# A two-layer S5 and gMLP trunk: the opening laid out anew, the S5 periods given less projection work, five y tiles prepared inside them

## The chip, the core and the metric

The kernel runs on one core of one Trainium2 chip. A core has five engines that run side by side, each through its own instructions in program order: TensorE (PE in the profile; its weight loads are PEld), VectorE (DVE), ScalarE (ACT), GpSimd (POOL) and SyncE (SP). An instruction that waits on a semaphore holds up everything behind it on its engine. DMAs are issued here by SP and, for a few transfers, by ScalarE; a DMA instruction also holds its engine until what it waits for has come. The metric is the device time of one execution in microseconds. The kernel before took 875.73 us (median of 3 runs, 874.96 to 876.68).

## What is computed

The reference runs two layers over a sequence of 1024 frames of 1024 features, all in float32, and a last rmsnorm:

```python
for i in range(DEPTH):                       # DEPTH = 2
    h = rmsnorm(x, norm_g[i])
    if i % 2 == 0:                           # S5 layer
        branch, gate = split(h @ s5_w_in)    # 1024 x 2048
        y = gelu(s5_mixer(branch, ...))      # 64 groups of 16 channels, 64 complex states each
        y = y * sigmoid(y @ w_glu + b_glu)
        out = (y * silu(gate)) @ s5_w_out
    else:                                    # gMLP layer
        u, v, gate = split(h @ sgu_w_in)     # 1024 x 3072
        out = (sgu_mixer(gelu(u), gelu(v), ...) * silu(gate)) @ sgu_w_out
    x = x + out
return rmsnorm(x, final_g)
```

The mixer is `h_t = lam_bar * h_(t-1) + b_bar @ u_t`, `y_t = Re(C h_t) + D u_t`, with a complex diagonal `lam_bar` that depends on the weights alone.

## The kernel before

Every large product is made from operands split in two float32r parts (hi and lo), with three matmuls for each tile of 128 rows: hi by hi, hi by lo, lo by hi. `w_split` makes the parts of a weight panel: a ScalarE copy (w_hi) and a subtraction on VectorE or GpSimd (w_lo).

The opening. x comes in two halves of 512 frames (tiles xh). `x_turn` transposes one 128-feature block of a half on TensorE (four transposes), `x_hi` copies it with the norm weight (ScalarE), `x_lo` takes the rest (VectorE); the results are ahi and alo. `in_mm(i, half, ks)` runs the matmuls of weight panel i against one half of the frames, one step for each of eight blocks k. The rms factor of a frame is multiplied in at the eviction (`in_out`, tile rb); `x_square`, `rsqrt` and `x_factor` make it for all eight blocks at once. Between these stand the operations on the mixer's parameters on VectorE (`decay`, `angles`, `powers`, taken one at a time by `pull`), and on GpSimd the phases (`phases`), the first table of rotations (`tab_ops(0)`, tile e) and the products of beta and B (`beta_b`, written to device memory as b_d and read back for each batch).

The S5 periods. The 64 groups are worked in 16 units of 4. `period(p)`, for p from -3 to 16, does one stage of several units, so that they overlap: kernel generation for unit p+3 (`gen_ops`, tiles wn and xn), transposes and the Toeplitz kernel for unit p+2 (`w_turn`, `k_mm`, `k_skip` into tile kpad, `k_store` from kpad to t_d), the recurrence of unit p, and the output product of unit p-1 (`out_mm`). The recurrence is a rotation by a table cs (`rot_co` on VectorE, `rot_si` on GpSimd), a real scan along time, and the rotation back. cs is a piece of e, brought by two SP DMAs in `load_cs`. All engines keep the order of the program text here. Into each period TensorE gets steps of the input projection as filling: `FILL` says how many at five places (11 in all; `FILL0` 6, for p below 0). In the periods `mm` takes steps from a list, `evict` runs one eviction, `split` one weight split, `queue` one weight load and one store; only two PSUM banks hold projection results then.

The tail. Units write their outputs to y_d. Each of 8 y tiles is loaded by eight DMAs (`load_y`), passed through gelu (`y_gelu`, ScalarE) and split (`y_split`, VectorE). `EARLY` of them (3) are prepared inside the last periods, the others behind them; then comes the gate product (w_glu), and the rest of the kernel, which the change leaves as it is. Both the y tiles and the gelu results use a pair of buffers (`ctile`) while the periods run.

Of the kernel before, what the change touches and what calls it, by code (L numbers as in the profile page):

```python
# [36 lines left out]
FILL = (3, 2, 2, 2, 2)  # L37
FILL0 = (2, 1, 1, 1, 1)
JR = 32
EARLY = 3  # L40
# [20 lines left out]
def trunk(ctx, tc, x, norm_g, final_g, s5_w_in, A_re, A_im, log_dt, B_re, B_im, C_re, C_im,  # L61
# [165 lines left out]
    b_d = drp.tile([KT, P, 8 * JR], F32, name="b_d")  # L227
# [3 lines left out]
    cnat = xp.tile([P, KT, 3, NS], F32, name="cnat")  # L231
    anat = tmp((G, 4, NS))
# [8 lines left out]
    ea = held.tile([P, 2, G], F32, name="ea")  # L241

# [31 lines left out]
    junk = stp.tile([P, D], F32, name="junk", tag="st")  # L274
# [5 lines left out]
    def x_factor(r):  # L280

        for half in range(2):
            ps = auxps()
            for b in range(4):
                dr = xp.tile([P, P], F32, name="dr", tag="dr", bufs=2)
                S.activation(dr, ident, AF.Copy, scale=r[:, half * 4 + b:half * 4 + b + 1])
                T.matmul(ps[:, b * P:(b + 1) * P], lhsT=ones, rhs=dr, start=True, stop=True)
            S.activation(rb[:, half * HALF:(half + 1) * HALF], ps, AF.Copy)
# [16 lines left out]
    def in_mm(i, half, ks):  # L305
        if ks[0] == 0:
            in_ps[i, half] = mmps()
        hi, lo = in_w[i]
        cs = slice(half * HALF, (half + 1) * HALF)
        for k in ks:  # L310
            mm3(in_ps[i, half], (hi[:, k], lo[:, k]), (ahi[:, k, cs], alo[:, k, cs]), k == 0, k == KT - 1)
# [118 lines left out]
    br, bi = tmp(), tmp()  # L430

    def vmul(orr, oi, ar_, ai_, br_, bi_, t, t2):
# [6 lines left out]
        yield tt(oi, oi, t2, ALU.add)  # L439

    def powers():

        l1r, l1i = lp[:, 0, :, 1], lp[:, 1, :, 1]
        tb, tc_ = tmp((P, G, L)), tmp((P, G, L))
        yield tt(l1r, ea[:, 0], cth[:, 0:G], ALU.mult)
        yield tt(l1i, ea[:, 0], sth[:, 0:G], ALU.mult)

        def beta():
            den, nr, t1, t2 = tmp(), tmp(), tmp(), tmp()
            yield tt(den, ar, ar, ALU.mult)  # L450
            yield tt(t1, ai, ai, ALU.mult)
# [64 lines left out]
    NB = {"wn": 2, "b0": 2, "xn": 5, "wt": 3, "e": 2, "cs": 3, "hh": 2, "traw": 3, "us": 4}  # L516
    tabs, wns, wts, xns, b0s, css, tts, us, hhs, gqs, rots, s1s, ggs, out_ps = ({} for _ in range(14))
# [206 lines left out]
    S.activation(warm, warm, AF.Square)  # L724
    Q.dma_start(g0, norm_g[0].rearrange("(k p) -> p k", p=P))
# [5 lines left out]
    w_load(1, xp.tile([P, KT, P], F32, name="raw_x"))  # L731
    load_x(1, 0, 2, 0, D)
    load_x(1, 2, 4, 0, D)
    load_bc()
# [27 lines left out]
    ps_a = auxps()
    for i in range(2):
        T.transpose(ps_a[:, i * G:(i + 1) * G], anat[:, 2 * i:2 * i + 2].rearrange("p a b -> p (a b)"), ident[0:G, 0:G])
    x_lo(0, 0)
    x_lo(0, 1)
    ts(ar, ps_a[:, 0:G], RE_CLIP, None, ALU.min)
    V.tensor_copy(ai, ps_a[:, G:2 * G])
    pull(2)
    x_lo(0, 2)  # L770
    pull(2)
    x_lo(0, 3)
    pull(2)
    w_split(0, V)
# [3 lines left out]
    x_square(0)  # L778
    x_square(1)
    pull(14)  # L780
    for k in range(4, 8):
# [8 lines left out]
    pull(64)  # L790
    phases()
    for _ in tab_ops(0):
        pass
    steps = powers()
# [8 lines left out]
    x_square(6)
    x_square(7)
    ts(xv, ss, 1.0 / D, RMS_EPS, ALU.mult, ALU.add)
    r = rsqrt(xv, KT, lambda: pull(1))
    x_factor(r)
    in_mm(1, 1, range(0, 4))
    c_turn(0)
    pull(8)  # L810
# [4 lines left out]
    w_load(2)
    in_mm(1, 1, range(4, 8))
    c_turn(1)
    pull(99)
    S.activation(bs, bs, AF.Copy, scale=sgn[:, 0:1])
    beta_b()  # L820
    w_split(2, V)
# [12 lines left out]
    todo = [(i, half, k) for i in range(2, 16) for half in range(2) for k in range(KT)]  # L834
    outs, splits, loads, stores = [], [3], [], []
# [39 lines left out]
    def period(p):  # L875
# [5 lines left out]
        if p % 2 == 0 and 2 <= p + 4 < 16:  # L881
            tab.append(tab_ops((p + 4) // 2))
# [43 lines left out]
        split()  # L926
# [13 lines left out]
    load_b0(0)  # L940
# [20 lines left out]
    for k in range(EARLY, KT):  # L961
        mm(5)
# [248 lines left out]
```

## Time and profile before

| | us |
|---|---|
| median of 3 runs | 875.73 |
| the profiled execution | 875.46 |
| its span (first to last instruction) | 873.7 |
| PE busy | 828.5 |
| DVE busy | 505.0 |
| ACT busy | 287.0 |
| POOL busy | 227.1 |

The span holds 10905 instructions; TensorE's mean granted clock is 0.977 of full speed. The chain of work that ended last is put down to PE for 76% of the span, DVE 12%, DMA 5%, ACT 3%. These are means over stages with different limits. A helper records each operation, so all instructions of the kernel carry one line number (L74) and are told apart by their tiles: mm is a projection product, aux another TensorE product, rot and cs the rotation, gg the scan's result, c a y tile or its gelu. The SP and ACT queues (SPq, ACTq) show DMAs by the time that issuing takes.

### The profile page before, as it was taken

To read this page: it belongs to the slowest core of one execution; us is meant where nothing else is said; L and a number is where in the kernel's file an instruction comes from. 1 tells how busy PE (TensorE), PEld (TensorE's weight loads), DVE (VectorE), ACT (ScalarE), POOL (GpSimd) and SP (SyncE) were. 2 spreads that over 40 slices of the span, in tenths; PEclk is the share of its full clock that TensorE was granted. 3 is DMA by queue.
4 is the path that set the end of the run, shared out by engine and by line. 5 is a ranking of instruction groups with operands and counts; after the bars stand their busy time and mean duration, and the time that the engine had idled before them with its cause. 6 is when DMAs were issued, how large, how long until landed. Compare 5 with 4: busy or idle time off the path is not lost.

```text
span 873.7 us, 10905 instructions
## 1 busy us (share of the span) xinstructions
PE 828.5 (95%) x3946; PEld 671.6 (77%) x3946; DVE 505.0 (58%) x1101; ACT 287.0 (33%) x519; POOL 227.1 (26%) x241
## 2 busy tenths in 40 slices
PE   5766999999999989999999999999999899999996
PEld 3555788888888768888888888888888688888884
DVE  5986788787744686665157511211399954462255
ACT  3622343443344564444112321311321122242122
POOL 1463776676542000000000000000036721212221
PEclk9978999999999979999999999999999999999999
DMA  9504887978877573456011321210310011371022
GB/s 255 74 26 126 219 230 199 254 190 222 213 181 180 139 236 97 145 168 217 25 73 72 121 73 49 97 48 1 97 49 0 25 49 32 137 225 40 2 97 96
DMA packets 124326, 104.35 MB, mean 119 GB/s; under 512 B 20592, under 2 KB 105584, under 8 KB 124272
## 3 DMA queue, kind: packets, MB, share of 16 engines
q1 hardware_dynamic: 114368, 97.29, 39.4%
q10 hardware_dynamic: 9904, 6.36, 2.3%
q8 instruction: 31, 0.51, 0.2%
q14 instruction: 23, 0.19, 0.1%
HBM read 68.50 MB, written 26.21 MB: 108 GB/s over the span
## 4 chain that ended last, share of the span: by engine, by line
PE 76%; DVE 12%; DMA 5%; ACT 3%; SPq 2%; issue 1%; POOL 1%; ACTq 0%; POOLq 0%
PE mm L74 67%; PE aux L74 7%; DVE lo L74 4%; SPq L74 2%; PE rot L74 1%; DMA c<-y_d 1%; DMA raw<-in_sgu_w_in 1%; DVE alo L74 1%; DVE t L74 1%; DMA raw<-in_s_w_in 1%; ACT c L74 1%; DVE rs_y L74 1%; DVE rs_t L74 1%; DVE stats L74 1%; DVE c L74 1%
## 5 line engine op out<-in xcount | busy, mean ns | idle before, releaser
L74 PE MATMUL mm<-ahi,w_hi 128*128 128x512 f32 x512 | 212.3, 415 | 4.9 <-ACT w_hi L74 4.1
L74 PE MATMUL mm<-ahi,w_lo 128*128 128x512 f32 x512 | 205.9, 402 | 3.1 <-DVE w_lo L74 3.1
L74 PE MATMUL mm<-alo,w_hi 128*128 128x512 f32 x512 | 204.6, 400 | 0.7 <-DVE alo L74 0.6
L74 PEld LDWEIGHTS mm<-ahi,w_hi 128*128 128x128 f32 x512 | 98.9, 193 | 26.7 <-ACT w_hi L74 4.6
L74 PEld LDWEIGHTS mm<-ahi,w_lo 128*128 128x128 f32 x512 | 98.6, 193 | 26.4 <-DVE w_lo L74 4.8
L74 PEld LDWEIGHTS mm<-alo,w_hi 128*128 128x128 f32 x512 | 99.0, 193 | 21.5 <-DVE alo L74 2.3
L74 PE MATMUL mm<-c,ahi 128*128 128x512 f32 x256 | 80.3, 395 | 0.0
L74 DVE TENSOR_TENSOR w_lo<-raw,w_hi 128x1024 fp32r<-128x1024 f32 x26 | 38.0, 1461 | 69.3 <-ACT w_hi L74 69.2
L74 POOL TENSOR_TENSOR lo<-lo,lnb 128x128 f32<-128x128 f32 x64 | 34.4, 566 | 162.1 <-DVE lo L74 162.1
L74 ACT ACTIVATE w_hi<-raw 128x1024 fp32r<-128x1024 f32 x39 | 41.1, 1054 | 82.1 <-PE mm L74 54.4
L74 DVE TENSOR_TENSOR c<-mm,c 128x512 f32<-128x512 f32 x32 | 22.0, 690 | 67.0 <-PE mm L74 67.0
L74 POOL TENSOR_SCALAR_AFFINE_SELECT wsn<-wsn 128x1024 f32<-128x1024 f32 x1 | 1.1, 1093 | 221.3 <-DMA wsn<-in_sgu_w_s 221.3
L74 PEld LDWEIGHTS mm<-c,ahi 128*128 128x128 f32 x256 | 48.1, 188 | 11.6
L74 PE MATMUL mm<-hi,w_hi 128*128 128x512 f32 x128 | 52.1, 408 | 2.8 <-DVE hi L74 1.7
L74 PE MATMUL mm<-lo,w_hi 128*128 128x512 f32 x128 | 52.7, 412 | 1.0 <-DVE lo L74 0.9
L74 PE MATMUL mm<-hi,w_lo 128*128 128x512 f32 x128 | 51.6, 404 | 0.0
L74 PE MATMUL mm<-hi,alo 128*128 128x512 f32 x128 | 51.0, 399 | 0.0
L74 PE MATMUL mm<-hi,ahi 128*128 128x512 f32 x128 | 50.7, 396 | 0.0
L74 PE MATMUL mm<-ahi,hi 128*128 128x512 f32 x128 | 50.6, 396 | 0.0
L74 PE MATMUL mm<-lo,ahi 128*128 128x512 f32 x128 | 50.6, 395 | 0.0
L74 PE MATMUL mm<-alo,hi 128*128 128x512 f32 x128 | 50.6, 395 | 0.0
L74 PE MATMUL mm<-c,alo 128*128 128x512 f32 x128 | 50.5, 395 | 0.0
(162 smaller groups left out, 1458.3 us busy)
## 6 DMA issues: line engine op xcount, KB each, us to landing
raw<-in_sgu_w_in SPq DMA_DIRECT2D x24, 512.0 KB, 3.7
cs<-e SPq DMA_DIRECT2D x32, 256.0 KB, 5.7
raw<-in_s_w_in SPq DMA_DIRECT2D x15, 512.0 KB, 4.5
u_d<-stage SPq DMA_DIRECT2D x8, 512.0 KB, 5.2
us<-u_d SPq DMA_DIRECT2D x16, 256.0 KB, 5.3
t_d<-kpad SPq DMA_DIRECT2D x64, 64.0 KB, 3.2
traw<-t_d SPq DMA_DIRECT2D x16, 256.0 KB, 5.5
y_d<-ysb ACTq DMA_DIRECT2D x16, 256.0 KB, 3.3
```

The lines of the kernel that those rows point to most:

```text
L74: ins = getattr(self.engine, name)(*args, **kwargs)
```

## The change

The constants and the order of work change; a few tiles move to other pools, and the beta products stay on chip.

```diff
-FILL = (3, 2, 2, 2, 2)
-FILL0 = (2, 1, 1, 1, 1)
+FILL = (2, 2, 2, 2, 1)
+FILL0 = (2, 2, 2, 1, 1)
+WARM = 16
-EARLY = 3
+EARLY = 5
...
+    def x_scale(half, r):
+        drs = [xp.tile([P, P], F32, name="dr", tag=f"dr{b}") for b in range(4)]
+        for b in range(4):
+            S.activation(drs[b], ident, AF.Copy, scale=r[:, b:b + 1])
+        return drs
+
+    def x_factor(half, drs):
+        ps = auxps()
+        for b in range(4):
+            T.matmul(ps[:, b * P:(b + 1) * P], lhsT=ones, rhs=drs[b], start=True, stop=True)
+        S.activation(rb[:, half * HALF:(half + 1) * HALF], ps, AF.Copy)
...
         for k in ks:
-            mm3(in_ps[i, half], (hi[:, k], lo[:, k]), (ahi[:, k, cs], alo[:, k, cs]), k == 0, k == KT - 1)
+            T.matmul(ps, lhsT=hi[:, k], rhs=ahi[:, k, cs], start=k == 0, stop=False)
+            T.matmul(ps, lhsT=hi[:, k], rhs=alo[:, k, cs], start=False, stop=False)
+        for k in ks:
+            T.matmul(ps, lhsT=lo[:, k], rhs=ahi[:, k, cs], start=False, stop=k == KT - 1)
...
-    def beta_b():
...
-        Q.dma_start(b_d.rearrange("b p x -> p b x"), b0.rearrange("p (b g) h -> p b (g h)", g=8))
+    def make_b0(b):
+        gs = slice(b * 8, (b + 1) * 8)
+        shb = [P, 8, HG]
+        bv = b0p[b % 2][:, :, 0:HG]
+        GP.tensor_tensor(bv, br[:, gs].unsqueeze(2).broadcast_to(shb), bn[:, gs], ALU.mult)
+        GP.tensor_tensor(b0t, bi[:, gs].unsqueeze(2).broadcast_to(shb), bs[:, gs], ALU.mult)
+        GP.tensor_tensor(bv, bv, b0t, ALU.add)
...
-    NB = {"wn": 2, "b0": 2, "xn": 5, "wt": 3, "e": 2, "cs": 3, "hh": 2, "traw": 3, "us": 4}
+    NB = {"wn": 2, "xn": 5, "wt": 3, "e": 2, "cs": 2, "hh": 2, "traw": 3, "us": 4}
...
         for g in range(8):
-            Q.dma_start(yt[g * HG:(g + 1) * HG]...
+            (Q if g % 2 else S).dma_start(yt[g * HG:(g + 1) * HG]...
```

The opening's program text behind the first half (the order before stands in the listing above):

```diff
+    r = rsqrt(x_var(0), 4, pull)
     for k in range(8):
         x_turn(1, k)
         x_hi(1, k)
+        if k == 3:
+            dr0 = x_scale(0, r)
         x_lo(1, k)
-    in_mm(0, 1, range(KT))
+        in_mm(0, 1, [k])
+    for n in range(4, 8):
+        x_square(n)
+    x_factor(0, dr0)
+    w_split(2, V)
...
+    in_mm(1, 1, range(KT))
     in_out(0, 0)
     in_out(1, 0)
+    pull(8)
+    r = rsqrt(x_var(1), 4, pull)
+    dr1 = x_scale(1, r)
...
+    x_factor(1, dr1)
+    in_mm(2, 0, range(KT))
+    w_split(3, V)
...
+    c_turn(0)
+    in_mm(2, 1, range(KT))
+    pull(99)
+    make_b0(0)
+    phases()
+    c_turn(1)
+    in_mm(3, 0, range(KT))
```

The periods and the y tiles inside them:

```diff
-        if p % 2 == 0 and 2 <= p + 4 < 16:
-            tab.append(tab_ops((p + 4) // 2))
+        if p % 2 == 0 and 2 <= p + 2 < 16:
+            tab.append(tab_ops((p + 2) // 2))
...
         if next_:
             load_u(p + 2)
-            load_cs(p + 2)
...
         mm(n[3])
-        split()
+        split(GP if p >= 0 else V)
+        if 0 <= p + 1 < 15:
+            load_cs(p + 1)
...
-            load_b0((p + 4) // 2)
+            make_b0((p + 4) // 2)
...
+    load_cs(15)
...
-    load_y(0)
-    for k in range(EARLY):
-        period(14 + k)
+    def prep(k):
+        load_y(k)
         y_gelu(k)
         y_split(k)
-        if k + 1 < EARLY:
-            load_y(k + 1)
+
+    for k in range(3):
+        period(14 + k)
+        for i in range(2 * k, min(2 * k + 2, EARLY)):
+            prep(i)
...
-        mm(5)
+        mm(KT)
```

`WARM` transposes of the identity run on TensorE ahead of x. In the first half of the opening, the copies and splits of a block follow each other without the `pull` steps between them, and w_lo of panel 0 goes to GpSimd.

What this does to the order of the engines shows at three places. First SP in two periods of the kernel before (us is the input of a unit, cs its table, t_d its Toeplitz kernel going out from kpad and traw the same coming back, u_d a stored panel; unit u has t_d number 132 + u):

```order
37 L74 DMA us<-u_d_117 128x4x128
38 L74 DMA cs<-e 64x1024 x2
39 L74 DMA traw<-t_d_134 128x4x128
40 L74 DMA t_d_135<-kpad_166 128x1x128 x4
41 L74 DMA raw<-in_s_w_in 128x8x128
42 L74 DMA u_d_119<-stage 128x1024
43 L74 DMA us<-u_d_118 128x4x128
44 L74 DMA cs<-e 64x1024 x2
45 L74 DMA traw<-t_d_135 128x4x128
46 L74 DMA t_d_136<-kpad_165 128x1x128 x4
```

and in the same two periods now:

```order
36 L75 DMA us<-u_d_117 128x4x128
37 L75 DMA traw<-t_d_134 128x4x128
38 L75 DMA t_d_135<-kpad_166 128x1x128 x4
39 L75 DMA cs<-e 64x1024 x2
40 L75 DMA raw<-in_s_w_in 128x8x128
41 L75 DMA u_d_121<-stage 128x1024
42 L75 DMA us<-u_d_118 128x4x128
43 L75 DMA traw<-t_d_135 128x4x128
44 L75 DMA t_d_136<-kpad_165 128x1x128 x4
45 L75 DMA cs<-e 64x1024 x2
```

The two cs loads have moved from ahead of the t_d stores of the period to behind them, and they bring the table of the next unit instead of that of the unit after it.

Second PE at the beginning of the opening's second half (xh the second half of x, aux its transposes, mm the products of panel 0). Before:

```order
52 L74 MATMUL aux<-ident,xh_150 128x128 x32
53 L74 MATMUL mm<-ahi,w_hi 128x512
54 L74 MATMUL mm<-alo,w_hi 128x512
55 L74 MATMUL mm<-ahi,w_lo 128x512
56 L74 MATMUL mm<-ahi,w_hi 128x512
57 L74 MATMUL mm<-alo,w_hi 128x512
```

Now, the first two of eight blocks:

```order
43 L75 MATMUL aux<-ident,xh_149 128x128 x4
44 L75 MATMUL mm<-ahi,w_hi 128x512
45 L75 MATMUL mm<-alo,w_hi 128x512
46 L75 MATMUL mm<-ahi,w_lo 128x512
47 L75 MATMUL aux<-ident,xh_149 128x128 x4
48 L75 MATMUL mm<-ahi,w_hi 128x512
49 L75 MATMUL mm<-alo,w_hi 128x512
50 L75 MATMUL mm<-ahi,w_lo 128x512
```

The 32 transposes stood together ahead of the products; now each block's four stand behind the products of the block before.

Third ScalarE behind unit 14's rotation (c<-y_d x4 is half of a y tile's eight loads, c<-c is a gelu, s and rot the swaps of unit 15, ysb an output). Before:

```order
143 L74 ACT_TABLE_LOAD
144 L74 ACTIVATE c<-c 128x512 x2
145 L74 ACTIVATE s_2611<-rot 64x512 x2
146 L74 ACTIVATE rot<-gg 64x512 x2
147 L74 ACTIVATE w_hi<-raw 128x1024
148 L74 ACTIVATE ysb<-aux 128x512
```

Now:

```order
143 L75 DMA c<-y_d_124 16x8x128 x4
144 L75 ACT_TABLE_LOAD
145 L75 ACTIVATE c<-c 128x512 x2
146 L75 DMA c<-y_d_125 16x8x128 x4
147 L75 ACTIVATE c<-c 128x512 x2
148 L75 ACTIVATE s_2657<-rot 64x512 x2
149 L75 ACTIVATE rot<-gg 64x512 x2
150 L75 ACTIVATE ysb<-aux 128x512
```

Two y tiles with their loads now stand between the periods where one gelu stood.

## Rows read from the trace of the kernel before

**Rows 1.** Windows by stage: stretch, its length, busy us (instructions), PEclk, DMA share, GB/s.

```profile
0.00:94.10 94.10, 65.12 (x273) 48.85 (x274) 67.87 (x172) 35.64 (x62) 39.79 (x64) 0.87 0.52 125
94.10:251.40 157.30, 156.50 (x952) 129.17 (x951) 124.87 (x225) 63.14 (x118) 100.60 (x75) 1.00 0.82 219
251.40:311.00 59.60, 56.75 (x269) 45.45 (x267) 33.12 (x60) 28.09 (x32) 9.98 (x6) 0.97 0.69 169
```

**Rows 2.** Timeline of PE: start us, us, engine, operation, out<-in [idle before <-releaser].

```profile
151.12 0.40 PE L74 MATMUL mm<-ahi,w_lo 128*128 128x512 f32 x1
151.35 0.40 PE L74 MATMUL mm<-ahi,w_hi 128*128 128x512 f32 x1
```

**Rows 3.** Timeline of DVE: units 0, 5 and 14.

```profile
96.47 0.70 DVE L74 TENSOR_TENSOR rot<-rot,cs 128x512 f32<-128x512 f32 x1 [0.33 <-ACT s L74]
...
152.15 0.70 DVE L74 TENSOR_TENSOR rot<-rot,cs 128x512 f32<-128x512 f32 x1 [0.55 <-ACT s L74]
...
154.81 1.35 DVE L74 TENSOR_TENSOR_SCAN gg<-ea,rot 128x128 f32<-128x128 f32 x4
157.70 0.23 DVE L74 SCALAR_TENSOR_TENSOR kpad<-eyej,dskip,aux 128x16 f32<-128x16 f32 x1 [1.54 <-ACT kpad L74]
...
253.73 0.70 DVE L74 TENSOR_TENSOR rot<-rot,cs 128x512 f32<-128x512 f32 x1 [4.06 <-ACT s L74]
```

**Rows 4.** Timeline of ACT in the same period.

```profile
156.26 1.22 ACT L74 ACTIVATE rot<-gg 64x512 f32<-64x512 f32 x2 [2.29 <-DVE gg L74]
```

**Rows 5.** Timeline of SP in the same period.

```profile
153.91 1.27 SPq L74 DMA_DIRECT2D cs<-e  x2
...
157.96 3.27 SPq L74 DMA_DIRECT2D t_d<-kpad  x4
```

**Rows 6.** The chain, start us, us, what; then all cs loads (tile view).

```profile
96.83 4.95 DMA cs<-e
...
DMA to landing us min/median/max: 3.7/5.7/7.7
```

**Rows 7.** Timeline of PE in the opening.

```profile
8.76 3.04 PE L74 MATMUL aux<-ident,xh 128*128 128x128 f32 x13 [0.24 <-DMA xh<-in_x]
...
33.10 1.91 PE L74 MATMUL aux<-ident,xh 128*128 128x128 f32 x16
35.27 0.66 PE L74 MATMUL aux<-ident,xh 128*128 128x128 f32 x4 [0.25 <-DVE alo L74]
```

**Rows 8.** Timeline of DVE in the opening.

```profile
26.68 1.21 DVE L74 TENSOR_TENSOR w_lo<-raw_x,w_hi 128x1024 fp32r<-128x1024 f32 x1
...
34.46 0.75 DVE L74 SCALAR_TENSOR_TENSOR alo<-aux,g,ahi 128x512 fp32r<-128x512 f32 x1 [1.32 <-ACT ahi L74]
...
64.31 0.68 DVE L74 TENSOR_TENSOR mu<-lp,t 128x512 f32<-128x512 f32 x1
```

**Rows 9.** Timeline of ACT in the opening.

```profile
42.21 1.05 ACT L74 ACTIVATE junk<-xh 128x1024 f32<-128x1024 f32 x1
```

**Rows 10.** Timeline of POOL in the opening: the phases' first and the table's last operation.

```profile
33.08 0.46 POOL L74 COPY ph<-t 128x64 f32<-128x64 f32 x2 [27.07 <-DVE t L74]
...
53.13 1.26 POOL L74 TENSOR_TENSOR e<-e,et 128x512 f32<-128x512 f32 x1
```

**Rows 11.** Timeline of PE after a wait, and the first gate panel's last product.

```profile
84.83 0.42 PE L74 MATMUL aux<-xn,b 128*32 128x128 f32 x8 [2.43 <-DMA b<-b_d]
...
86.34 0.63 PE L74 MATMUL mm<-ahi,w_hi 128*128 128x512 f32 x1
86.77 0.63 PE L74 MATMUL mm<-alo,w_hi 128*128 128x512 f32 x1
...
310.23 0.63 PE L74 MATMUL mm<-hi,w_lo 128*128 128x512 f32 x1
```

**Rows 12.** Timeline of SP in the tail.

```profile
275.62 27.64 SPq L74 DMA_DIRECT2D c<-y_d  x48
```

**Rows 13.** DMA issues (page, part 6): count, KB each, median us to landing.

```profile
c<-y_d SPq DMA_DIRECT2D x64, 64.0 KB, 3.3
```

**Rows 14.** Timeline of ACT in the tail: one gelu, two halves.

```profile
262.01 2.15 ACT L74 ACTIVATE c<-c 128x512 f32<-128x512 f32 x2
```

More of the change, by code (lines that the diff above doesn't have):

```diff
@@ L241, in trunk @@
     ea = held.tile([P, 2, G], F32, name="ea")
+    br, bi = (held.tile([P, G], F32, name=c) for c in ("br", "bi"))
+    b0p = [held.tile([P, 8, JR], F32, name=f"b0_{i}") for i in range(2)]
+    b0t = held.tile([P, 8, HG], F32, name="b0t")
     def load_x(half, b0, b1, c0, c1):
@@ L278, in x_square, with x_var @@
         S.activation(junk, xh[n // 4][:, n % 4], AF.Square, accum_out=ss[:, n:n + 1])
[L280 to L288, printed above, removed]
+    def x_scale(half, r):
[8 more added lines that the diff above has]
+        S.activation(rb[:, half * HALF:(half + 1) * HALF], ps, AF.Copy)
+    def x_var(half):
+        hs = slice(half * 4, half * 4 + 4)
+        ts(xv[:, hs], ss[:, hs], 1.0 / D, RMS_EPS, ALU.mult, ALU.add)
+        return xv[:, hs]
     in_w, in_st, in_ps, in_raw = {}, {}, {}, {}
@@ L438, in vmul @@
         yield tt(orr, orr, t, ALU.subtract)
-        yield tt(oi, oi, t2, ALU.add)
+        yield last.tensor_tensor(oi, oi, t2, ALU.add)
     def powers():
@@ L523, in tab_ops @@
     def tab_ops(b):
-        e = per.tile([P, 2, UG, 8, 16], F32, name="e", bufs=NB["e"])
-        t = per.tile([P, UG, 8, 16], F32, name="et")
+        e = pool["gen"].tile([P, 2, UG, 8, 16], F32, name="e", bufs=NB["e"])
+        t = pool["gen"].tile([P, UG, 8, 16], F32, name="et")
         sh = [P, UG, 8, 16]
@@ L730, in trunk @@
     load_x(0, 2, 4, HALF, D)
[L731 to L734, printed above, removed]
+    w_load(1, raw_x)
+    for c in range(2):
+        for b in (0, 2):
+            load_x(1, b, b + 2, c * HALF, (c + 1) * HALF)
     GP.memset(ph[:, 0, :, 0:1], 1.0)
@@ L740, in trunk @@
         GP.memset(kp[:, 0:(L - 1) * HG], 0.0)
+    for b0 in b0p:
+        GP.memset(b0[:, :, HG:JR], 0.0)
     GP.memset(sg[0:NS], 1.0)
@@ L749, in trunk @@
     GP.tensor_copy(anat[:, 3], anat[:, 2])
+    ps_a = auxps()
+    for _ in range(WARM):
+        T.transpose(ps_a[:, HALF - P:HALF], ident, ident)
+    for i in range(2):
+        T.transpose(ps_a[:, i * G:(i + 1) * G], anat[:, 2 * i:2 * i + 2].rearrange("p a b -> p (a b)"), ident[0:G, 0:G])
     for _ in exp(dt, ldt, (P, G)):
@@ L761, in trunk @@
         x_hi(0, k)
[L762 to L774, printed above, removed]
+        x_lo(0, k)
+        if k == 1:
+            w_split(0, GP)
     in_mm(0, 0, range(0, 4))
@@ L777, in trunk @@
         x_turn(0, k)
[L778 to L781, printed above, removed]
         x_hi(0, k)
         x_lo(0, k)
-        pull(3)
+    for k in range(4, 8):
         in_mm(0, 0, [k])
+    w_load(2)
+    load_b()
+    x_square(0)
     w_split(1, V)
-    for n in range(2, 6):
+    for n in range(1, 4):
         x_square(n)
     in_mm(1, 0, range(KT))
[L790 to L794, printed above, removed]
+    w_load(3, raw_x)
+    load_c()
+    pull(12)
+    r = rsqrt(x_var(0), 4, pull)
     for k in range(8):
@@ L798, in trunk @@
         x_hi(1, k)
+        if k == 3:
+            dr0 = x_scale(0, r)
         x_lo(1, k)
-        if k < 4:
-            pull(3)
-    in_mm(0, 1, range(KT))
[L803 to L810, printed above, removed]
+        in_mm(0, 1, [k])
[3 more added lines that the diff above has]
+    w_split(2, V)
+    w_load(4)
+    load_small()
+    in_mm(1, 1, range(KT))
     in_out(0, 0)
     in_out(1, 0)
+    pull(8)
+    r = rsqrt(x_var(1), 4, pull)
+    dr1 = x_scale(1, r)
+    S.activation(bs, bs, AF.Copy, scale=sgn[:, 0:1])
+    pull(99)
+    steps = powers()
+    x_factor(1, dr1)
+    in_mm(2, 0, range(KT))
+    w_split(3, V)
     in_out(0, 1)
     in_store(0)
[L815 to L821, printed above, removed]
     in_out(1, 1)
     in_store(1)
-    w_load(3)
+    c_turn(0)
+    in_mm(2, 1, range(KT))
+    pull(99)
+    make_b0(0)
+    phases()
+    c_turn(1)
+    in_mm(3, 0, range(KT))
     xp_cm.__exit__(None, None, None)
@@ L831, in trunk @@
     banks.update(mm=[0, 1], aux=[2, 3], rot=[4, 5], gq=[6], tv=[7])
-    todo = [(i, half, k) for i in range(2, 16) for half in range(2) for k in range(KT)]
-    outs, splits, loads, stores = [], [3], [], []
+    todo = [(i, half, k) for i in range(3, 16) for half in range(2) for k in range(KT)
+            if (i, half) != (3, 0)]
+    outs, splits, loads, stores = [(2, 0), (2, 1), (3, 0)], [4], [], []
     def mm(n):
@@ L888, in period @@
             load_u(p + 2)
-            load_cs(p + 2)
+        if p == 0:
+            for _ in gen:
+                pass
         if here:
@@ L936, in period @@
             put_powers((p + 4) // 2)
-            load_b0((p + 4) // 2)
+            make_b0((p + 4) // 2)
     put_powers(0)
-    load_b0(0)
+    for _ in tab_ops(0):
+        pass
     for p in range(-3, 14):
         period(p)
+    load_cs(15)
     gen_cm.__exit__(None, None, None)
```

36 lines of the change are left out of this document (15 added, 21 removed).

## The prediction

> **What bounds the kernel now.** I read the stages first, since the shares over the whole span mix stages with different limits [rows 1]. From 94.1 to 251.4 us, the S5 periods, PE is busy 156.5 of 157.3 us at granted clock 1.00: nothing but PE sets their pace. In the opening, 0 to 94.1 us, PE is busy 65.1 us, so 29 us of it are idle, and the granted clock is 0.87. From 251.4 to 311 us, where the last periods, the y tiles and the first gate panel lie, PE is busy 56.75 of 59.6 us. The rest of the kernel is not touched.
>
> Then the timeline of one period. On PE matmuls of 512 columns start 0.23 us apart, so one step of the input projection (three of them) costs 0.69 us [rows 2]. On VectorE the rot<-rot,cs of unit 0 starts at 96.47 and that of unit 14 at 253.73: 14 periods in 157.26 us, 11.23 us each [rows 3]. Inside one: rot at 152.15, the scan ends at 154.81 + 1.35 = 156.16, kpad at 157.70 [rows 3]. kpad is late because ScalarE first swaps the scan's result back (2 x 64x512, 1.22 us from 156.26) and only then copies kpad [rows 4]. On SP the four t_d stores start at 157.96, right behind kpad, and take 3.27 us; the cs loads had been issued at 153.91, ahead of them [rows 5]. So the t_d issue hangs on this period's scan, and what SP has in program order behind it hangs on it too.
>
> **The change, part by part.**
>
> The periods. FILL falls from 11 to 9 steps: 2 x 0.69 = 1.37 us less PE work, which alone would make a period 11.23 - 1.37 = 9.86 us. But load_cs moves. Before, period p loads the table of unit p+2 ahead of the t_d stores, with a whole period to spare. Now period p loads that of unit p+1 behind them, and unit p+1 multiplies by it at the top of the next period. This closes a ring: scan of p, swap, kpad, four t_d issues, two cs issues, landing, rot of p+1, scan of p+1. Its length: rot to end of scan 156.16 - 152.15 = 4.0; end of scan to first t_d 157.96 - 156.16 = 1.8; t_d 3.27 when the queue is loaded, 2.5 if no issue waits, I take 3.0 [rows 3, 5]; half of the pair of cs issues (1.27), 0.65 [rows 5]; landing 4.95 in the one place where it ended the chain, least 3.7, median 5.7 [rows 6], and I take 4.5, since the queue is emptier in a longer period and close to the chain's row. Sum 13.95 us; bounds 4.0 + 1.8 + 2.5 + 0.6 + 3.7 = 12.6 and 4.0 + 1.8 + 3.3 + 0.8 + 5.7 = 15.6. Even the lower bound is longer than the 11.23 us that a period takes now. The ring runs 14 times (cs of units 1 to 14, the last pair goes together); units 0 and 13 save about 0.5 us each between rot and scan, having no kernel generation there. 14 x 13.95 - 1 = 194.3 us against 157.3: **+37 us** (from +19 to +61). The PE work taken out of the periods is then worth nothing, PE being no longer late.
>
> The Trainium skill, "DMA: Bandwidth & Descriptors", section "Anatomy of one DMA — SWDGE (gpsimd) path", fits a transfer as about 2.0 us plus bytes over 436 GB/s, for the path that GpSimd issues; for 256 KB that is 2.6 us, an estimate. The row here shows 4.95 us, and no cs load below 3.7 [rows 6]. By the rule the ring would be 12.05 us and my total 14 x 1.9 = 26.6 us lower, 923.
>
> The beta load that stood on SP (b_d) goes, and three small GpSimd products in every second period take its place. GpSimd has idle time in every period and after its last product only SP's weight load waits, which stands behind cs: nothing, either way. The y loads that go to the ScalarE queue are priced in the tail.
>
> The opening. 24 more projection steps (56 instead of 32) and 6 more in the three filling periods lie ahead of unit 0. Its first half gets faster. The transposes start at 8.76 as before, being bound by x [rows 7]; with no recurrence step of VectorE between the splits, and w_lo of panel 0 on GpSimd, I get the products of blocks 0 to 3 at 15.5, 4 to 7 at 19.7, and after the split of panel 1 (1.2 us [rows 8]) the 24 products of panel 1 at 26.3, where they end at 33.10 now [rows 7]. The second half gets slower. Now 32 transposes stand on PE ahead of all products; in the new order each block's four transposes wait for the products of the block before, and those for its copy and split. One turn is from 33.10 to the end of the split, 34.46 + 0.75 = 35.21, and then two matmuls with a cold start, 0.56: 2.7 us [rows 7, 8]; eight turns 21.9 us, to 48.5, with PE busy some 1.1 us of each 2.7. The last copy is then at T = 47.
>
> From T on it is a chain: four squares at 1.18 with the accumulator read [rows 9], the factor copy 0.6, w_hi and w_lo of panel 2 2.3, two strided evictions 2.1, eight recurrence steps 1.6, the second rsqrt with its steps 3.1: T+14.4. PE, which ended panel 1 at T+8, waits for the diagonal copies until T+16.3. Then w_hi, w_lo of panel 3 and two evictions to T+21.9, and the powers: 38 operations, from 0.14 us to the 0.60 us of mu [rows 8], 9.5 us; with the GpSimd add and the copy of the powers T+33. Kernel generation, three evictions and w_lo of panel 4 bring the first free bank for panel 3's second half at T+40. From there PE and VectorE wait for each other once per filling period (2 banks): 27.5 us to the table of unit 0, of which 8 us are its own ring (t_d, cs, landing). GpSimd's phases and first table take 21 us now (33.08 to 54.4 [rows 10]) and stand behind mu; that ends at T+55 and stays hidden. So unit 0's rot is at 47 + 67.5 = 114.5, and with 1.5 us for matmuls that run slow after the waits 116, against 96.47 [rows 3]: **+20 us** (from +12 to +30).
>
> The tail. Now from unit 14's rot at 253.73 to the last product of the first gate panel, 310.86, it is 57.1 us [rows 3, 11], and SP's y loads, 48 issues in 27.64 us, feed it [rows 12]. Each y tile was loaded a period before its gelu. In the new order the load stands directly ahead of its gelu on ScalarE, twice in a row, and one buffer pair makes the second load wait for the first gelu. So ScalarE stands still for issue (4 x 0.55, half of the eight) plus landing 3.3 [rows 13], then gelu 2.15 [rows 14]: about 7.5 us per tile. In order after rot 14: scan, swap, split, output and store 9 us; two tiles to 23.6; unit 15's swap, scan, swap, output to 31; two tiles to 46.3; split and output 48.3; tile 4 to 55; twelve issues to 62; three gelus, a weight split and a sigmoid with two table loads of 1.3 between them to 72; split and last products 74. PE's work in this stretch (50 steps, 34 us) lies beside it. **+17 us** (from +6 to +21).
>
> Sum: 20 + 37 + 17 = +74 us. The profiled execution is 875.46 us (span 873.7), the median of the runs shown 875.73; the sum is made on the former and gives 949.5, so 949.
>
> **The rivals.**
>
> The cs load comes sooner. For it: in a 14 us period SP has idle time before kpad, and the least landing is 3.7 [rows 6]. Against it: t_d's own packets are just ahead of it. Ring 12.6 us: 949 - 19 = 930.
>
> The opening ends no later than now. For it: the second rsqrt ran beside GpSimd and takes less without; PE idles 29 us there [rows 1]. Against it: the eight turns and the wait at T+8 are plain in the order. 949 - 20 = 929.
>
> PE becomes late as well. At the slow level a 512-column matmul is recorded with 0.63 us instead of 0.40, and starts every 0.43, after a wait of 2.4 us [rows 2, 11]; a ring of 14 us leaves PE a gap of 2 to 4 us in each period. 27 matmuls at 0.43 and the small ones (11.23 - 33 x 0.23 = 3.6 us now) at double are 18.8 us, so a period between 14 and 18.8, say 16: 949 + 29 = 978. The Trainium skill, "TensorE: Matmul & The Clock Gate", section "HAM oscillation — how this bites in real kernels", describes a loop that waits for a DMA in each pass and comes back at the low clock each time. In this trace no period waits so, its granted clock being 1.00 [rows 1].
>
> Faster: the ring does not bind. Then a period is 9.86 us, 14 of them 19 us less, and if the opening absorbs its 30 steps (20.6 us) in its 29 us of idle and costs 9 more, it ends at 866. It decides where the load lands within 9.86 - 4.0 - 1.8 - 3.0 - 0.65 = 0.4 us of its issue; break-even with 11.23 us is at 1.8. The least landing here is 3.7 [rows 6], so this holds only if SP does not stand still at t_d, and it does: no t_d issue ahead of kpad [rows 3, 5].
>
> **How the numbers follow.** Forecast 0.58, load sooner 0.12, opening no later 0.14, PE late too 0.12, the ring does not bind 0.04. The range must hold the first three and most of the fourth: the ring's bounds alone give 931 to 973, the opening's another 8 down and 10 up, the tail's 11 down, not all at once: 908 to 978. Runs of this kernel differ by about 0.2%, which is what counts as no change. Only the last case is not slower; of its 0.04 I give 0.03 to faster and 0.01 to no change.
>
> **What would show it.** Right: periods of 13 to 15 us between rot<-rot,cs starts, VectorE idle before it with the cs load as releaser, t_d directly ahead of cs on SP; eight gaps of some 1.6 us on PE between 26 and 49 us, a gap of about 8 us ahead of the second x_factor; ScalarE idle on c<-y_d four to five times for 3 us or more. Wrong: periods near 10 us with rot released by ScalarE or PE; unit 0's rot before 100 us; the last products of the first gate panel less than 60 us behind unit 14's rot.

## The result and the profile after

The changed kernel takes 967.63 us (median of 4 runs, 965.23 to 970.48) against 875.35 us: ratio 1.1058, 95% interval 1.102 to 1.1096. The profiled execution took 965.23 us, its span 963.5. I cut both traces at three events that both have: unit 0's rot<-rot,cs, unit 14's, and the end of the last gate product (w_glu). Windows of the kernel after, then the last two of the kernel before, columns as in [rows 1]:

```profile
0.00:121.21 121.21, 99.80 (x415) 75.39 (x416) 70.19 (x195) 38.05 (x66) 31.19 (x63) 0.83 0.48 117
121.21:312.85 191.64, 155.09 (x893) 124.44 (x891) 115.69 (x213) 60.73 (x116) 108.60 (x96) 0.94 0.62 158
312.85:482.44 169.59, 129.89 (x537) 103.38 (x538) 89.90 (x147) 67.85 (x91) 9.91 (x6) 0.87 0.52 132
482.44:963.50 481.06, 469.95 (x2120) 383.96 (x2119) 221.70 (x560) 120.72 (x248) 76.49 (x97) 0.99 0.22 74
```

```profile
253.73:393.20 139.47, 135.66 (x592) 108.54 (x591) 91.14 (x147) 66.30 (x89) 9.98 (x6) 0.96 0.58 160
393.20:873.70 480.50, 468.87 (x2121) 382.98 (x2119) 221.13 (x559) 120.69 (x248) 76.73 (x97) 0.99 0.22 74
```

With unit 0 at 96.47 and unit 14 at 253.73 before [rows 3], the opening costs 24.7 us, the 14 periods 34.4, the tail 30.1 and the rest 0.6: 89.8 us together, the difference of the spans.

One period of the kernel after, on VectorE and then on SP, answers to [rows 3, 5]:

```profile
189.26 0.70 DVE L75 TENSOR_TENSOR rot<-rot,cs 128x512 f32<-128x512 f32 x1 [4.57 <-DMA cs<-e]
...
191.92 1.35 DVE L75 TENSOR_TENSOR_SCAN gg<-ea,rot 128x128 f32<-128x128 f32 x4
...
194.81 0.23 DVE L75 SCALAR_TENSOR_TENSOR kpad<-eyej,dskip,aux 128x16 f32<-128x16 f32 x1 [0.57 <-ACT kpad L75]
...
202.75 0.70 DVE L75 TENSOR_TENSOR rot<-rot,cs 128x512 f32<-128x512 f32 x1 [3.78 <-DMA cs<-e]
```

```profile
195.06 3.07 SPq L75 DMA_DIRECT2D t_d<-kpad  x4
198.23 1.19 SPq L75 DMA_DIRECT2D cs<-e  x2
```

rot is released by the cs load. Before, it was released by ScalarE's swap.

In the opening, the turns of the second half on PE (a turn is a block's four transposes, its copy and split, and its three products), then the windows on either side of the fall of the granted clock, which lies in the fourth turn, answer to [rows 7, 8]:

```profile
26.92 0.60 PE L75 MATMUL aux<-ident,xh 128*128 128x128 f32 x4
28.29 0.50 PE L75 MATMUL mm<-ahi,w_hi 128*128 128x512 f32 x1 [0.78 <-ACT ahi L75]
29.08 0.50 PE L75 MATMUL mm<-alo,w_hi 128*128 128x512 f32 x1 [0.28 <-DVE alo L75]
29.42 0.40 PE L75 MATMUL mm<-ahi,w_lo 128*128 128x512 f32 x1
29.66 0.60 PE L75 MATMUL aux<-ident,xh 128*128 128x128 f32 x4
...
38.31 1.06 PE L75 MATMUL aux<-ident,xh 128*128 128x128 f32 x4
40.14 0.80 PE L75 MATMUL mm<-ahi,w_hi 128*128 128x512 f32 x1 [0.78 <-ACT ahi L75]
...
64.61 2.08 PE L75 MATMUL aux<-dr,ones 128*128 128x128 f32 x8 [3.22 <-ACT dr L75]
...
90.25 0.47 PE L75 MATMUL mm<-ahi,w_hi 128*128 128x512 f32 x1 [3.44 <-DVE stage L75]
```

```profile
27.08:36.50 9.42, 5.46 (x25) 3.15 (x23) 2.27 (x4) 2.80 (x5) 0.00 (x0) 1.00 0.96 194
36.50:52.87 16.37, 13.26 (x32) 7.79 (x32) 3.74 (x5) 5.69 (x11) 0.00 (x0) 0.50 0.00 0
```

The first three turns are 2.74 us long (26.92 to 29.66), as forecast. The fourth, in which the clock falls, takes 3.18, and the last four (38.31 to 52.87) take 3.64 each, at granted clock 0.50, the level of 1.2 GHz.

In the tail, ScalarE's loads and gelus of the five tiles answer to [rows 14]:

```profile
319.59 1.98 ACTq L75 DMA_DIRECT2D c<-y_d  x4
330.15 1.28 ACT L75 ACT_TABLE_LOAD   x1 [10.99 <-DMA c<-y_d]
331.45 2.04 ACT L75 ACTIVATE c<-c 128x512 f32<-128x512 f32 x2
...
339.46 2.05 ACT L75 ACTIVATE c<-c 128x512 f32<-128x512 f32 x2 [5.97 <-DMA c<-y_d]
...
355.86 2.17 ACT L75 ACTIVATE c<-c 128x512 f32<-128x512 f32 x2 [7.74 <-DMA c<-y_d]
...
363.94 2.05 ACT L75 ACTIVATE c<-c 128x512 f32<-128x512 f32 x2 [5.91 <-DMA c<-y_d]
...
377.33 1.12 ACT L75 ACTIVATE c<-c 128x512 f32<-128x512 f32 x1 [9.92 <-DMA c<-y_d]
```

ScalarE stands still on all five tiles; the idle time counts from its last work, issue and landing together.

### The profile page after: what moved, and what is told of

It reads as the page before. It is cut to its first block, busy times and chain, and to the rows that moved or that the text cites. A ratio compares the mean times of both kernels' runs of the same rounds, so it can differ in the third digit from the quotient of the medians.

```text
span 963.5 us, 10961 instructions
## 1 busy us (share of the span) xinstructions
PE 854.7 (89%) x3962; PEld 687.2 (71%) x3962; DVE 497.5 (52%) x1112; ACT 287.4 (30%) x521; POOL 226.2 (23%) x262
## 4 chain that ended last, share of the span: by engine, by line
PE 56%; DMA 13%; DVE 12%; issue 9%; ACT 4%; SPq 4%; POOL 2%; ACTq 1%; DVEq 0%; POOLq 0%
PE mm L75 52%; DMA cs<-e 4%; SPq L75 4%; DMA c<-y_d 4%; PE aux L75 3%; DVE lo L75 3%; DMA traw<-t_d 3%; DVE rot L75 2%; DVE gg L75 1%; ACT c L75 1%; DMA raw<-in_sgu_w_in 1%; DVE tv L75 1%; DVE wn L75 1%; ACT rot L75 1%; DVE stats L75 1%
## 5 line engine op out<-in xcount | busy, mean ns | idle before, releaser
L75 PE MATMUL mm<-ahi,w_hi 128*128 128x512 f32 x512 | 222.3, 435 | 50.9 <-ACT rot L75 21.1
L75 PE MATMUL mm<-alo,w_hi 128*128 128x512 f32 x512 | 212.0, 414 | 0.9 <-DVE alo L75 0.9
L75 PE MATMUL mm<-ahi,w_lo 128*128 128x512 f32 x512 | 203.3, 410 | 0.8 <-POOL w_lo L75 0.8
L75 PEld LDWEIGHTS mm<-ahi,w_hi 128*128 128x128 f32 x512 | 102.9, 201 | 79.1 <-ACT rot L75 21.6
L75 PEld LDWEIGHTS mm<-alo,w_hi 128*128 128x128 f32 x512 | 103.1, 201 | 23.9 <-DVE alo L75 4.6
L75 PEld LDWEIGHTS mm<-ahi,w_lo 128*128 128x128 f32 x512 | 101.7, 199 | 24.2 <-POOL w_lo L75 1.5
L75 PEld LDWEIGHTS mm<-c,ahi 128*128 128x128 f32 x256 | 48.1, 188 | 11.6
L75 ACT ACTIVATE rot<-gg 64x512 f32<-64x512 f32 x32 | 19.1, 596 | 125.0 <-DVE gg L75 124.5
L75 DVE TENSOR_TENSOR rot<-rot,cs 128x512 f32<-128x512 f32 x32 | 22.3, 697 | 56.3 <-DMA cs<-e 51.7
L75 PE MATMUL mm<-hi,w_lo 128*128 128x512 f32 x128 | 50.7, 400 | 0.5 <-DVE w_lo L75 0.5
L75 PE MATMUL mm<-hi,ahi 128*128 128x512 f32 x128 | 50.7, 396 | 0.0
L75 PE MATMUL mm<-ahi,hi 128*128 128x512 f32 x128 | 50.7, 396 | 0.0
```

The lines of the kernel that those rows point to most:

```text
L75: ins = getattr(self.engine, name)(*args, **kwargs)
```

## The experiments

Times, and events in each profile (us; rot 0 and rot 14 are the rot<-rot,cs of units 0 and 14, a period is a fourteenth of the way from the one to the other, the tail runs from rot 14 to the last gate product). The times of before, after, e1, e7, e8 and e11 are medians of 4 runs or more, the others single runs; the ten runs of e7 lie 1.1% apart at most.

| kernel | time | rot 0 | period | tail |
|---|---|---|---|---|
| before | 875.35 | 96.5 | 11.23 | 139.5 |
| after | 967.63 | 121.2 | 13.69 | 169.6 |
| e1 | 940.81 | 120.0 | 11.97 | 170.2 |
| e2 | 916.95 | 123.6 | 10.15 | 169.3 |
| e3 | 914.72 | 101.1 | 13.72 | 139.6 |
| e4 | 947.19 | 103.1 | 13.82 | 168.2 |
| e5 | 939.74 | 121.5 | 13.80 | 143.4 |
| e6 | 935.17 | 121.3 | 13.87 | 137.2 |
| e7 | 873.18 | 101.6 | 10.16 | 146.3 |
| e8 | 864.26 | 100.8 | 10.33 | 134.9 |
| e9 | 915.11 | 120.5 | 10.28 | 169.7 |
| e10 | 973.84 | 122.5 | 13.78 | 175.3 |
| e11 | 862.54 | 101.1 | 10.33 | 137.3 |
| e12 | 953.10 | 121.3 | 13.72 | 159.3 |

**The periods: e1, e2, e3, e9.** My theory is the ring through the cs load. e1 moves the load ahead of t_d:

```diff
-        if p % 2 == 0 and 2 <= p + 2 < 16:
-            tab.append(tab_ops((p + 2) // 2))
+        if p % 2 == 0 and 2 <= p + 4 < 16:
+            tab.append(tab_ops((p + 4) // 2))
...
             load_u(p + 2)
+        if 0 <= p + 1 < 15:
+            load_cs(p + 1)
...
-        if 0 <= p + 1 < 15:
-            load_cs(p + 1)
```

> The changed kernel with one thing put back: the table of unit p+1 is loaded at the top of period p, ahead of the t_d stores, and the tables are formed two periods earlier as before. Ring theory (table load behind t_d closes a ring through the scan): the periods fall from 13.69 us to what PE needs, 9.9 us by my sum, at most 10.5; unit 0's rot to unit 14's rot 138 to 147 us instead of 191.6; total 912 to 921. Rival A (the store and load back of the Toeplitz kernel, t_d then traw, sets the pace, the cs load only stands in the queue with it): periods stay above 12 us, total above 940. Rival B (PE is late by its lowered clock): granted clock in the periods stays near 0.93 and periods above 11 us, total above 927.

A miss: periods of 11.97 us, alternating between short and long. SP and GpSimd of e1 in a long one:

```profile
167.99 2.09 SPq L75 DMA_DIRECT2D cs<-e  x2
```

```profile
176.12 1.07 POOL L75 TENSOR_TENSOR e<-ph 128x512 f32<-128x512 f32 x1 [8.45 <-DMA cs<-e]
177.15 1.26 POOL L75 TENSOR_TENSOR hh<-gg,cs 128x512 f32<-128x512 f32 x1
```

My edit had made a wait of its own. GpSimd forms the table after next in the buffer from which the load just issued still reads; it stands 8.45 us for that load, and hh, which the rotation back needs, stands behind it. e9 keeps e1's place of the load and begins the tables a period later:

```diff
-        if p % 2 == 0 and 2 <= p + 4 < 16:
-            tab.append(tab_ops((p + 4) // 2))
+        if p % 2 == 1 and 2 <= p + 3 < 16:
+            tab.append(tab_ops((p + 3) // 2))
```

> The kernel of e1 (table load of unit p+1 at the top of period p) with the tables of rotations begun one period later, so that GpSimd writes over a table no sooner than a period after the last load from it was issued. If e1 missed its time because GpSimd's table product waited there for the load just issued from the same buffer: periods 10.0 to 10.4 us, unit 0's rot to unit 14's 140 to 146 us, total 912 to 922, as in e2. Rival (a load of unit p+1 is too late wherever it stands): periods stay near 12 us, total near 940.

10.28 us and 915.11, as expected: the buffer was e1's reason, and ahead of t_d the load of unit p+1 is soon enough. e2 leaves the load behind t_d, but for unit p+2. Its tables are begun as in the kernel before, unlike what its expectation says of them:

```diff
-    NB = {"wn": 2, "xn": 5, "wt": 3, "e": 2, "cs": 2, ...
+    NB = {"wn": 2, "xn": 5, "wt": 2, "e": 2, "cs": 3, ...
...
-            tab.append(tab_ops((p + 2) // 2))
+            tab.append(tab_ops((p + 4) // 2))
...
-        if 0 <= p + 1 < 15:
-            load_cs(p + 1)
+        if next_:
+            load_cs(p + 2)
...
-    load_cs(15)
```

> The changed kernel with the table load left behind the t_d stores, but for unit p+2 instead of p+1 (three cs buffers, two wt buffers, tables formed as in the changed kernel). Ring theory: the place on SP does not matter once there is a period of slack, so periods 9.9 to 10.5 us and total 912 to 921, as with the load moved ahead. Rival (SP's queue itself is too long in that order, whatever the unit): periods stay above 12 us, total above 940.

10.15 us and 916.95, as expected. VectorE's waits in the periods of e2 (for what, us, times, longest):

```profile
DVE kpad L75 <- ACT kpad L75: 17.3, 14, 1.5
DVE rot L75 <- POOL s L75: 3.6, 4, 1.8
DVE rot L75 <- ACT s L75: 1.1, 2, 0.5
```

No wait for cs is left. So the ring needs both, the place behind t_d and the missing period of slack: e9 takes away the one, e2 the other, and either is enough. e3 puts the ring into the kernel before, where PE has 11 steps a period:

```diff
-            tab.append(tab_ops((p + 4) // 2))
+            tab.append(tab_ops((p + 2) // 2))
...
             load_u(p + 2)
-            load_cs(p + 2)
...
         split()
+        if 0 <= p + 1 < 15:
+            load_cs(p + 1)
...
+    load_cs(15)
```

> The kernel before with only the table load moved as in the change (unit p+1, behind the t_d stores; tables formed two periods later). Ring theory: periods of 13.4 to 14 us although PE work stays 11.2 us, unit 0's rot to unit 14's 187 to 196 us instead of 157.3, total 905 to 915. Rival (the lengthening in the changed kernel comes from the lighter filling and its PE gaps, not from the load): periods within 0.5 us of 11.2, total under 885.

```profile
154.90 0.70 DVE L74 TENSOR_TENSOR rot<-rot,cs 128x512 f32<-128x512 f32 x1 [3.58 <-DMA cs<-e]
...
168.62 0.70 DVE L74 TENSOR_TENSOR rot<-rot,cs 128x512 f32<-128x512 f32 x1 [2.95 <-DMA cs<-e]
```

13.72 us a period and 914.72, as expected (VectorE of e3, above). With 9 steps it was 13.69: the ring sets the period, and two steps of PE more or less do not change it.

**The opening: e4.**

```diff
     for k in range(8):
...
         x_lo(1, k)
-        in_mm(0, 1, [k])
+    in_mm(0, 1, range(KT))
```

> The changed kernel with the products of panel 0 with the second half behind all eight blocks' transposes and splits, instead of block by block. Theory (the eight turns cost PE and VectorE about 14 to 16 us of the opening): last copy near 35 us instead of 50, unit 0's rot near 106 (104 to 110) instead of 121.2, total 949 to 955. Rival (GpSimd's products, phases and first table, or the second factor, end last whatever the turns do): unit 0's rot stays above 117, total above 960.

Unit 0 at 103.1, 18.1 us sooner, 947.19 us: slightly more than expected. The turns alone took the opening from 103 to 121. The clock, which fell to 0.50 at 36.5 us in the changed kernel, is 1.00 from 26 to 45 us in e4.

**The tail: e5, e6, e10, e12.** e5 puts all y loads on SP, each one tile ahead; e6 takes the end of the kernel before (three tiles, one a period):

```diff
-            (Q if g % 2 else S).dma_start(yt...
+            Q.dma_start(yt...
...
+    load_y(0)
     def prep(k):
-        load_y(k)
         y_gelu(k)
+        if k + 1 < EARLY:
+            load_y(k + 1)
         y_split(k)
```

> The changed kernel with all y loads on SP and each issued one tile ahead: the first before period 14, the next right behind the gelu of the tile before. Theory (ScalarE stands still on loads that are issued directly ahead of their gelu; the tail is 30 us longer for that): the waits of tiles 0, 2 and 4 (11.0, 7.7 and 9.9 us) go, those of tiles 1 and 3 stay at 6 to 8 us since two gelus stand in a row; the tail from unit 14's rot to the last gate product shrinks from 169.6 us to 145 to 155 (139.5 before), total 942 to 952. Rival (the five tiles inside the periods are one stop of ScalarE too many whatever the loads do): tail stays above 160 us, total above 956.

> The changed kernel with the end of before: three tiles inside the periods, one behind each of the last three, each loaded a period ahead on SP; five tiles behind them with eight projection steps each. Theory: the tail comes back to what it was, 136 to 144 us from unit 14's rot to the last gate product, total 932 to 941. Rival (the tail is longer because the projection steps that the lighter periods left over land in it): tail stays above 150 us, total above 946.

143.4 and 137.2 us: both tails came back, e5's a little more than expected. e5 changes the queue and the time of issue at once, so their shares are not told apart. In it the second tile of a pair still waits (7.0 and 5.7 us). Why the waits were longer than I had them is the question of e10 (all eight loads on ScalarE) and e12 (SP's weight load and z_d store, `queue()`, taken out of the last three periods by a flag and put behind the tiles' loads):

```diff
-            (Q if g % 2 else S).dma_start(yt...
+            S.dma_start(yt...
```

> The changed kernel with all eight loads of a y tile on ScalarE's queue instead of four there and four on SP. If the long waits (11.0 and 9.9 us at tiles 0 and 4) come from the half that stands on SP behind a weight load and a z_d store: these two waits fall to 4 to 6 us, the four more issues cost 2 us of ScalarE a tile, tail 155 to 165 us instead of 169.6, total 952 to 962. Rival (the landing itself is that slow after the y_d store just ahead, on whichever queue): tail 168 to 180, total 964 to 976.

```diff
-        period(14 + k)
+        period(14 + k, False)
         for i in range(2 * k, min(2 * k + 2, EARLY)):
             prep(i)
+        queue()
```

> The changed kernel with the weight load and the z_d store of each of the last three periods issued behind the y tiles' loads instead of ahead of them. In the changed kernel ScalarE waits 11.0 us for tile 0 and 9.9 us for tile 4, where 512 KB transfers of SP are in the air with the loads, and 5.9 to 6.0 us for tiles 1 and 3, where none is. If these transfers (in the air, and ahead on SP) make the difference: the waits of tiles 0 and 4 fall to 5.5 to 7.5 us, tail 160 to 166 us instead of 169.6, total 956 to 963. Rival (the y_d store ahead of the loads on ScalarE's queue makes it): the waits stay at 9.5 us or more, total 964 to 972.

ScalarE in e10, tiles 0 and 4, then in e12 the same:

```profile
322.23 4.99 ACTq L75 DMA_DIRECT2D c<-y_d  x8
332.28 1.28 ACT L75 ACT_TABLE_LOAD   x1 [10.49 <-DMA c<-y_d]
...
370.55 4.01 ACTq L75 DMA_DIRECT2D c<-y_d  x8
382.86 1.12 ACT L75 ACTIVATE c<-c 128x512 f32<-128x512 f32 x1 [12.75 <-DMA c<-y_d]
```

```profile
320.19 1.91 ACTq L75 DMA_DIRECT2D c<-y_d  x4
324.50 1.28 ACT L75 ACT_TABLE_LOAD   x1 [4.83 <-DMA c<-y_d]
...
360.42 2.04 ACTq L75 DMA_DIRECT2D c<-y_d  x4
366.47 1.10 ACT L75 ACTIVATE c<-c 128x512 f32<-128x512 f32 x1 [6.49 <-DMA c<-y_d]
```

e10 comes out in its rival's range: on one queue the waits are as long. Of them 5.0 and 4.0 us are the issuing of eight loads, where four took 2.0. e12 takes the 11.0 and 9.9 us of the changed kernel down to 4.8 and 6.5 and the tail to 159.3, a little more than expected, though the y_d store still stands ahead on ScalarE's queue; so that store is not the reason. But e12 changes two things: SP's half of tile 0's loads also goes out sooner, at 313.19 instead of 322.22, since it no longer stands behind a weight load that waits for its buffer (8.4 us for GpSimd's w_lo).

The landings of single loads in e10 tell the two apart. SP's weight load, then tile 0's loads on ScalarE's queue issued ahead of it and behind it (the tile view of c in two windows):

```profile
323.78 0.38 SPq L75 DMA_DIRECT2D raw<-in_s_w_in  x1
```

```profile
L75 ACTq DMA_DIRECT2D c<-y_d x3: 442/458/517, 322.2 to 323.3; - x3
DMA to landing us min/median/max: 2.5/2.6/2.7
...
L75 ACTq DMA_DIRECT2D c<-y_d x5: 441/504/1343, 323.8 to 326.7; - x5
DMA to landing us min/median/max: 5.2/6.3/7.0
```

No load of this tile stands on SP there, and yet those issued with or behind SP's 512 KB weight load, which a z_d store of 512 KB follows at 324.26, take about twice as long or more. The eight loads of tile 1, with no such transfer beside them, land in 2.3 to 2.7 us. So the transfers on their way are a reason by themselves. How much of the 11.0 and 9.9 us the place on SP adds in the changed kernel, no run tells.

**All undone: e7, e8, e11.** e7 is e2, e4 and e5 in one kernel, e8 is e2, e4 and e6.

> The changed kernel with the table load one period ahead (cs for unit p+2), panel 0's second products behind all transposes, and the y loads one tile ahead. If the three causes add: unit 0's rot near 103, periods 10.1 us, unit 14's rot near 245, tail 145 to 155: total 868 to 878, against 873.4 for the kernel before. Rival (the causes cover one another, so that removing all gives less than the sum): above 885.

> As the one before, with the end of the kernel before in place of the one-ahead loads. If the causes add: unit 14's rot near 245, tail 136 to 144, total 859 to 867, faster than the kernel before (873.4) by 0.7 to 1.6%. Rival (less PE work inside the tail's periods makes the y tiles the bound there): tail above 148, total above 871.

e7 comes out level with the kernel before (ratio 0.9982, 0.9957 to 1.0006). e8 is faster than both: 0.9884 (0.9841 to 0.9928), 1.2% under the kernel before. By times, e2, e4 and e6 (single runs) take 50.7, 20.4 and 32.5 us off the changed kernel, 103.6 together; e8 takes off 103.4. The three causes do not cover one another. Windows of e8:

```profile
0.00:100.83 100.83, 85.23 (x412) 67.10 (x413) 69.48 (x195) 37.31 (x66) 39.19 (x70) 0.95 0.59 144
100.83:245.47 144.64, 138.01 (x859) 113.68 (x859) 115.31 (x214) 60.97 (x116) 100.78 (x89) 1.00 0.81 205
245.47:380.37 134.90, 129.66 (x575) 103.84 (x574) 90.91 (x147) 66.55 (x90) 9.92 (x6) 0.99 0.65 168
```

It is 4.4 us later at unit 0 than the kernel before, with 30 more projection steps behind it, and takes the 14 periods in 144.6 us instead of 157.3. e11 tries the one long wait left in e8's first half:

```diff
+    r = rsqrt(x_var(1), 4, pull)
     x_factor(0, dr0)
+    dr1 = x_scale(1, r)
     w_split(2, V)
...
     pull(8)
-    r = rsqrt(x_var(1), 4, pull)
-    dr1 = x_scale(1, r)
```

> e8 with the second half's factor (rsqrt and diagonal copies) formed directly behind the squares, ahead of the weight split and the two evictions that PE does not wait for as early. In e8 PE stands 3.58 us for it. If that wait is on the path: unit 0's rot 2 to 3.5 us sooner, total 860 to 862 (e8: 864.3 median). Rival (the evictions, now 2 us later, free their banks as late as the factor came before): within 1 us of e8.

PE in e8, then in e11:

```profile
45.09 1.37 PE L75 MATMUL aux<-dr,ones 128*128 128x128 f32 x8 [3.58 <-ACT dr L75]
...
70.42 0.76 PE L75 MATMUL mm<-ahi,w_hi 128*128 128x512 f32 x1 [4.12 <-DVE stage L75]
```

```profile
43.90 0.47 PE L75 MATMUL mm<-ahi,w_hi 128*128 128x512 f32 x1 [0.63 <-ACT rb L75]
...
70.70 0.76 PE L75 MATMUL mm<-ahi,w_hi 128*128 128x512 f32 x1 [8.30 <-DVE stage L75]
```

The 3.58 us are gone and stand again at the next bank, where 4.12 became 8.30; unit 0 is no sooner. 0.9859 (0.9826 to 0.9893) overlaps with e8, so no gain of e11 over e8 is shown.

## Why the prediction was right, point by point

- **The ring.** Right, and shown by e2, e3 and e9. Of its terms: rot to end of scan 4.0, then 1.8 to t_d, t_d 3.1, all as taken. Half the cs pair and the landing came to 202.75 - 198.23 = 4.5 us where I had 0.65 + 4.5 = 5.15. That makes 13.5 us for the period shown; others run up to 14.8, so that the mean is 13.69 against 13.95, and +34.4 us against +37. cs lands with a least of 3.0 and a median of 3.8 us here. My reason for taking less than 5.7, a queue emptier in a longer period, was wrong: in e2 the median is 3.8 us as well, in periods of 10.15. The estimate of 2.6 us by the Trainium skill, "DMA: Bandwidth & Descriptors", section "Anatomy of one DMA — SWDGE (gpsimd) path", is still below both; that page speaks of GpSimd's path, and these loads are SP's.
- **PE without the ring** was to need 9.86 us a period. e2 shows 10.15; PE is busy 135.5 of its 142.05 us there, so it waits some 0.5 us in each period. The rival in which the ring does not bind was priced at 866 us with no term for the tail; e2, without the ring but with the opening and the tail as changed, takes 916.95.
- **PE late as well** did not happen: the granted clock was 0.94 in the periods, and of the 15 rot<-rot,cs of units 0 to 14, all but one waited for cs (51.7 us together) and one for PE (3.0).
- **The opening.** +24.7 against +20. Panel 1 ended at 27.1 (forecast 26.3). The first three turns took the 2.7 us forecast, the fourth 3.18 and the last four 3.64, together 4.0 us more, and the rest of my chain held from there in its sum (the last copy, T, at 51.0 instead of 47; first free bank at T+39, forecast T+40; unit 0 at T+70, forecast T+69). The term that was missing is the clock: I had looked for its fall in the periods, and it fell in the turns. In the first three PE waits twice in each, 0.78 us for ScalarE and 0.28 for VectorE, where I had forecast gaps of 1.6. In e4, without these waits, the clock did not fall there; that they are what brings it down is argued from that and not shown by itself. The Trainium skill, "TensorE: Matmul & The Clock Gate", section "HAM oscillation — how this bites in real kernels", tells of a loop that waits for a DMA in each pass and comes back at the low clock. The trace agrees in that PE waits in each pass and falls to 0.50; here the waits are for other engines and 0.78 us at most.
- **PE's wait at the second factor** was to be 8 us and was 3.2: PE came there later, at T+10.4 instead of T+8, on the slow clock, and the factor sooner, at T+13.6 instead of T+16.3. That the first free bank then came as forecast is partly luck.
- **The tail is the term that I mis-sized:** +17 us, bounds 6 to 21, measured +30.1, above the bounds (measured to the last gate product; I had counted to the end of the first gate panel). The first pair of tiles took 21.9 us (forecast 14.6), the second 17.4 (15.3), tile 4 11.6 (6.7): together 14.3 us, about what is missing. I had taken the landing from the median of a kernel in which these loads had time to spare [rows 13]. It holds for tiles 1 and 3, whose waits of 6.0 and 5.9 us are near the 5.5 of my sum; the loads of tiles 0 and 4 meet SP's weight loads and stores, as e10 and e12 show, and tile 0 has a table load of 1.28 us that I had left out. I had also laid the first gate panel's products beside this chain. They begin at 389.89, behind a weight split that stands on ScalarE behind tile 5's gelu.

Opening and tail together were 18 us low, the periods 3 high: 949 against 967.6 us. The three causes and the way each one works were as forecast; the size of the tail was not, and the total lies in the range because the range was wide enough for that.

## What to carry to other kernels

Before moving a load behind a store that waits for this step's result, write down whom the load feeds and when: if the next step needs it, the queue's order has closed a ring, and no work removed from the busiest engine shortens it (13.69 and 13.72 us with 9 and 11 steps). A step of slack (e2) or a place ahead of that store (e9) opens it; a buffer reused too early can close another ring, as in e1. Lighter periods and a longer opening were worth having (e8: 12.6 us less in the periods, 4.4 more in the opening) once the ring and the turns were undone and no load was issued directly ahead of its user on the engine that uses it.

## What the runs showed of the hardware that I had not expected

- The clock fell to 0.50 within the eight turns; in the 9.42 us before, at 1.00, PE was busy 5.46. In e4, without the turns, the opening up to unit 0 ran at 0.92 in the mean, in the changed kernel at 0.83.
- A y tile's eight loads of 64 KB held ScalarE 4.8 to 11.0 us from its last work on, by what else was on its way and by when SP's half was issued (e12, after). In e10 a single one landed in 2.5 to 2.7 us ahead of SP's 512 KB transfers and in 5.2 to 7.0 beside them.
- How soon cs lands goes by whether one of SP's 512 KB transfers (weight load, panel store) is on its way when it is issued, and not by the length of the period or the DMA share. Behind t_d none is: the median is 3.8 us, in periods of 13.69 us at a share of 0.62 (after) and of 10.15 us at 0.80 (e2) alike. At the top of a period it is 5.7 us, at 0.82 (before [rows 6]) and 0.77 (e9); counted load by load, 6.0 and 5.9 us with such a transfer on its way, 4.1 and 4.3 without.
